# Taking the token mean off the residual input: VectorE in three operations instead of GpSimd in seven

## The chip, the cores and the metric

The kernel runs on one core of one Trainium2 chip. What counts is the device time of one execution in microseconds (us), taken as the median of several runs. The core's engines each work through their own queue in order: TensorE (PE in the profile) multiplies matrices into PSUM, VectorE (DVE) and ScalarE (ACT) do element-wise work and reductions, GpSimd (POOL) does element-wise work too, and SyncE (SP) issues most of the DMA transfers. They wait for each other through semaphores.

## The reference, cut to what matters

Two decoder layers run over 256 tokens of 1024 features. Each has three sub-layers: a feed-forward block, a mixer, and a second feed-forward block. The mixer of the first layer ("even") runs a recurrent block and gated linear attention side by side; that of the second ("odd") is latent attention. After every sub-layer the input, scaled by ALPHA, is added to the gated output, and the sum is normalised over the features of each token.

```python
def layer_norm(x, g, b):
    mu = jnp.mean(xf, -1, keepdims=True)
    var = jnp.mean(jnp.square(xf - mu), -1, keepdims=True)
    return ((xf - mu) * lax.rsqrt(var + LN_EPS) * g + b).astype(x.dtype)

def deepnorm_residual(x, f, gate, g, b, weight=1.0):
    return layer_norm(DN_ALPHA * x + weight * (1 + gate[:, None, :]) * f, g, b)
...
for l in range(DEPTH):
    mod = c_act @ mod_w[l] + mod_b[l]
    sh1, sc1, g1, sh2, sc2, g2, sh3, sc3, g3 = jnp.split(mod, N_MOD, axis=-1)
    f = swiglu(modulate(x, sh1, sc1), ffn_in[l, 0], ffn_out[l, 0])
    x = deepnorm_residual(x, f, g1, ln_g[l, 0], ln_b[l, 0], 0.5)
    u = modulate(x, sh2, sc2)
    m = even_mixer(u, ...) if l % 2 == 0 else odd_mixer(u, positions, ...)
    x = deepnorm_residual(x, m, g2, ln_g[l, 1], ln_b[l, 1])
    f = swiglu(modulate(x, sh3, sc3), ffn_in[l, 1], ffn_out[l, 1])
    x = deepnorm_residual(x, f, g3, ln_g[l, 2], ln_b[l, 2], 0.5)
```

A layer norm gives the same result when any one number per token is first taken off all of that token's features. The kernel uses this: the number is the mean over the first 128 features, so that the squares it sums later are of small numbers.

## The kernel before, in words

**Layout.** Features lie on the 128 partitions and tokens along the free axis, so that the 1024 features are eight feature tiles of 128 x 256. `ax` holds the eight tiles of the scaled input, `yy` the eight tiles of the sum.

**Weights and products.** All weights come as one stream of 1 MB slabs (`wraw`), loaded by SP in the order in which TensorE uses them. Half a slab, 128x1024, is split for precision into a high part `whi` on ScalarE (L348) and a low part `wlo` on VectorE (L349), some four half slabs ahead of use. A product of one 128x128 weight block is three matmuls of 256 columns: high with high (L420), low activation with high weight (L421), high activation with low weight (L422). Half a slab thus feeds 24 matmuls. Between the splits VectorE also reduces slabs of the conditioning weights, half a slab each (`junk`, L398); they come in through the same buffers (`modw`).

**The end of a sub-layer** is the class `Boundary`, six times in the program. `f` counts the output tiles 0 to 7.

- L610 in `tile_out` reads a finished tile from PSUM, multiplies it by the gate and adds `ax` of that tile (VectorE). This frees the PSUM bank. L614 squares the result on ScalarE, L617 and L618 add tile and square to running sums on VectorE, and L584 (ScalarE) and L585 (VectorE) make a scaled high and low copy, `flat`, which the first matmuls of the next sub-layer ("early" ones) take before the statistics are known.
- `shift_out` is called halfway through the products of tile 1, when tile 0 has been added up. L593 rounds tile 0, an all-ones matmul (L595) gives each token its mean over tile 0, L598 copies that to `shift`, and from then on it must come off everything: off `yy` tile 0 by VectorE (L601) and off `ax` tiles 1 to 7 by GpSimd (L600), so that the sums of tiles 1 to 7 lack it as they are formed. L610 of tile f therefore waits for the subtraction of tile f.
- `stats` closes the boundary: two all-ones matmuls over the running sums (L626, L627) and two over tile 7 and its square (L628, L629).

**Three kinds of boundary.** A feed-forward output tile takes 22 products, 66 matmuls, so its tiles come slowly (four boundaries). In the odd mixer a tile takes 8 products, 24 matmuls. In the even mixer the eight tiles were half summed up earlier and lie two to a PSUM bank (`acc[f]`), and 8 products finish each.

**What sets the order.** A tile scheduler places the instructions on each engine from the data they need and from priorities; everything in the boundary quoted below stands under `tc.high_priority()`. Each engine then takes its own list in order, whatever is ready further back.

```python
yr = T(wk, [P, SEQ], F32R, tag="shift", bufs=1)        # L591
act.activation(yr, y, AF.Copy)                          # L593
pe.matmul(sp[:, :SEQ], ones_r, yr, start=True, stop=True)   # L595
act.activation(shift, sp[:, :SEQ], AF.Copy)             # L598
```

Of the kernel before, what the change touches and what calls it, by code (L numbers as in the profile page):

```python
# [16 lines left out]
AF = mybir.ActivationFunctionType  # L17
DVE, ACT, PE = mybir.EngineType.DVE, mybir.EngineType.Activation, mybir.EngineType.PE
ALU = mybir.AluOpType
MULT, ADD, SUB, MAX, MIN = ALU.mult, ALU.add, ALU.subtract, ALU.max, ALU.min  # L20

P = 128
DM = 1024
KD = DM // P
SEQ = 256
# [209 lines left out]
def trunk_kernel(ctx: ExitStack, tc: tile.TileContext, xT, cvec, pos, wst, modw, colsd,  # L235
                 rgw, wa2, outT):
    nc = tc.nc
    sync, act, vec, pool, pe = nc.sync, nc.scalar, nc.vector, nc.gpsimd, nc.tensor
# [10 lines left out]
    wk = ctx.enter_context(tc.tile_pool(name="wk", bufs=2))  # L249
# [6 lines left out]
    def nm(s):  # L256
        uid[0] += 1
        return f"{s}_{uid[0]}"

    def T(pl, shape, dt=F32, tag=None, **kw):  # L260
        return pl.tile(shape, dt, tag=tag, name=nm(tag), **kw)
# [12 lines left out]
    def axps():  # L274
        return T(ps_ax, [P, 512], tag="ax")
# [192 lines left out]
    ax = T(main, [P, KD, SEQ], tag="ax")  # L468
# [73 lines left out]
    class Boundary:  # L542
# [44 lines left out]
        def shift_out(self):  # L587


            y = self.y[:, 0, :]  # L590
            yr = T(wk, [P, SEQ], F32R, tag="shift", bufs=1)  # L591
            with tc.high_priority():
                act.activation(yr, y, AF.Copy)  # L593
            sp = axps()
            pe.matmul(sp[:, :SEQ], ones_r, yr, start=True, stop=True)  # L595
            shift = T(wk, [P, SEQ], tag="shift", bufs=1)
            with tc.high_priority():
                act.activation(shift, sp[:, :SEQ], AF.Copy)  # L598
                for j in range(1, KD):
                    pool.tensor_tensor(ax[:, j, :], ax[:, j, :], shift, SUB)  # L600
                vec.tensor_tensor(y, y, shift, SUB)  # L601
                ysq = T(wk, [P, SEQ], tag="ysq")
                act.activation(ysq, y, AF.Square)
                self.scaled(0)
            self.p0 = (y, ysq)

# [745 lines left out]
```

## Time and profile before

| | us |
|---|---|
| median of three runs | 1032.38 (1031.18, 1032.38, 1034.73) |
| the profiled execution | 1033.28 |
| its span, first to last instruction | 1031.5 |
| TensorE busy | 1001.4 |
| VectorE busy | 887.0 |
| ScalarE busy | 606.2 |
| GpSimd busy | 54.7 |

The mean granted TensorE clock over the span was 0.992.

How to read the lines that follow. In the list of groups a line gives the line of the program, the engine, the operation, the output and the inputs with their shapes, and behind the bar the busy time, the mean duration of one in ns, and the idle time of the engine ahead of them. In a timeline a line starts with start and duration in us; `x2` says that two neighbours are drawn as one, and a bracket gives the idle time ahead and what ended it. A line of a table by stretches (it starts with from:to) gives the length of the stretch and then the busy time of PE, PEld (loading of weights into TensorE), DVE, ACT, POOL and SP with their counts, the granted clock, the share of time in which the DMA engines were busy, and their GB/s. In these lines the buffers' numbers are left out, so that `mm`, a PSUM bank, does not say which tile.

### The profile page before, as it was taken

The numbers are of one execution on the slowest core, as the hardware profiler recorded it, in microseconds if no ns is written. First come the engines' busy times: TensorE is split into PE (matmuls) and PEld (weight loads), VectorE is DVE, ScalarE is ACT, GpSimd is POOL, SyncE is SP. The second block draws the span as 40 slices with busy tenths as digits, with TensorE's granted clock in tenths as the row PEclk, the third lists the DMA queues.
The fourth block names the chain that finished last, engine by engine and source line by source line (L and its number), as shares of the span: only waits on it lengthen the run. The fifth ranks groups of instructions, "written<-read, shape, count | busy, mean of one in ns | idle before, by whom it ended". The sixth has DMA issues, their size and how long they took to land.

```text
span 1031.5 us, 20651 instructions
## 1 busy us (share of the span) xinstructions
PE 1001.4 (97%) x8346; PEld 978.3 (95%) x8346; DVE 887.0 (86%) x1498; ACT 606.2 (59%) x1014; POOL 54.7 (5%) x70
## 2 busy tenths in 40 slices
PE   8999999999999989999999999999999999999995
PEld 6999999998989979999999999999999889999995
DVE  5889999798999789999897899999888799666664
ACT  3646664678886656645545674454568666545442
POOL 0000011000000020000030000003000200000200
PEclk9999999999999999999999999999999999999998
DMA  9998798655566924799976479987743236666411
GB/s 345 415 349 323 272 347 313 232 203 193 196 247 258 346 98 170 261 377 377 363 290 251 165 261 371 344 330 324 286 164 123 83 127 255 237 240 244 166 41 41
DMA packets 38578, 258.57 MB, mean 251 GB/s; under 512 B 4289, under 2 KB 6849, under 8 KB 7762
## 3 DMA queue, kind: packets, MB, share of 16 engines
q1 hardware_dynamic: 37330, 256.20, 66.3%
q8 instruction: 65, 1.06, 0.4%
q10 hardware_dynamic: 1152, 1.05, 0.3%
q14 instruction: 31, 0.25, 0.1%
HBM read 256.18 MB, written 1.05 MB: 249 GB/s over the span
## 4 chain that ended last, share of the span: by engine, by line
PE 82%; DVE 11%; ACT 3%; issue 2%; DMA 2%; POOL 0%; SPq 0%; ACTq 0%; DVEq 0%
PE mm L420 25%; PE mm L422 25%; PE mm L421 25%; DVE wlo L349 3%; DVE junk L398 2%; DMA rgt<-rgw 1%; DMA wraw<-modw 1%; PE mm L1022 1%; PE mm L1021 1%; PE mm L1023 1%; ACT whi L348 1%; PE ax L422 1%; PE ax L421 1%; PE ax L420 1%; DVE acc L618 0%
## 5 line engine op out<-in xcount | busy, mean ns | idle before, releaser
L349 DVE TENSOR_TENSOR wlo<-wraw,whi 128x1024 fp32r<-128x1024 f32 x338 | 412.1, 1228 | 76.4 <-ACT whi L348 75.5
L420 PE MATMUL mm<-uhi,whi 128*128 128x256 f32 x1660 | 458.3, 278 | 7.9 <-ACT whi L348 3.6
L421 PE MATMUL mm<-ulo,whi 128*128 128x256 f32 x1660 | 458.7, 277 | 0.5 <-DVE ulo L463 0.5
L422 PE MATMUL mm<-uhi,wlo 128*128 128x256 f32 x1660 | 456.4, 277 | 0.5 <-DVE wlo L349 0.5
L348 ACT ACTIVATE whi<-wraw 128x1024 fp32r<-128x1024 f32 x338 | 353.6, 1056 | 171.9 <-PE mm L421 139.0
L420 PEld LDWEIGHTS mm<-uhi,whi 128*128 128x128 f32 x1660 | 311.3, 188 | 9.9 <-ACT whi L348 4.4
L421 PEld LDWEIGHTS mm<-ulo,whi 128*128 128x128 f32 x1660 | 312.3, 188 | 1.0 <-DVE ulo L463 0.7
L422 PEld LDWEIGHTS mm<-uhi,wlo 128*128 128x128 f32 x1660 | 311.5, 188 | 0.8 <-DVE wlo L349 0.7
L422 PE MATMUL mm<-hhi,wlo 128*128 128x256 f32 x704 | 194.5, 276 | 0.8 <-DVE wlo L349 0.8
L421 PE MATMUL mm<-hlo,whi 128*128 128x256 f32 x704 | 194.3, 276 | 0.0
L420 PE MATMUL mm<-hhi,whi 128*128 128x256 f32 x704 | 194.3, 276 | 0.0
L398 DVE CUSTOM_DVE_ANT_0 junk<-wraw,cact,cols 128x1024 bf16<-128x1024 f32 x144 | 186.4, 1294 | 7.3 <-DMA wraw<-modw 6.7
L422 PEld LDWEIGHTS mm<-hhi,wlo 128*128 128x128 f32 x704 | 132.2, 188 | 1.0 <-DVE wlo L349 1.0
L420 PEld LDWEIGHTS mm<-hhi,whi 128*128 128x128 f32 x704 | 132.2, 188 | 0.0
L421 PEld LDWEIGHTS mm<-hlo,whi 128*128 128x128 f32 x704 | 132.2, 188 | 0.0
L600 POOL TENSOR_TENSOR ax<-ax,shift 128x256 f32<-128x256 f32 x42 | 47.9, 1173 | 840.8 <-ACT shift L598 667.2
L462 ACT ACTIVATE hhi<-h 128x256 fp32r<-128x256 f32 x88 | 35.7, 413 | 61.2 <-DVE h L731 60.9
L614 ACT ACTIVATE ysq<-yy 128x256 f32<-128x256 f32 x42 | 17.4, 414 | 60.8 <-DVE yy L610 58.8
L610 DVE SCALAR_TENSOR_TENSOR yy<-mm,gate,ax 128x256 f32<-128x256 f32 x48 | 22.9, 478 | 17.7 <-PE mm L422 16.5
L731 DVE SCALAR_TENSOR_TENSOR h<-mm,sg 128x256 f32<-128x256 f32 x75 | 30.8, 416 | 8.1 <-PE mm L422 8.1
L463 DVE TENSOR_TENSOR hlo<-h,hhi 128x256 fp32r<-128x256 f32 x88 | 35.8, 415 | 0.0
L442 ACT ACTIVATE sg<-mm 128x256 f32<-128x256 f32 x75 | 27.5, 367 | 4.2 <-PE mm L422 3.0
(296 smaller groups left out, 1103.4 us busy)
## 6 DMA issues: line engine op xcount, KB each, us to landing
wraw<-wst SPq DMA_DIRECT2D x169, 1024.0 KB, 5.2
wraw<-modw SPq DMA_DIRECT2D x71, 1024.0 KB, 7.1
wraw<-modw SPq DMA_DIRECT2D x2, 512.0 KB, 5.3
rgt<-rgw ACTq DMA_DIRECT2D x8, 128.0 KB, 4.6
yy<-xT SPq DMA_DIRECT2D x8, 128.0 KB, 9.2
wraw<-wst SPq DMA_DIRECT2D x2, 512.0 KB, 6.4
outT<-yy SPq DMA_DIRECT2D x3, 256.0 KB, 2.7
outT<-yy SPq DMA_DIRECT2D x2, 128.0 KB, 2.7
```

The lines of the kernel that those rows point to most:

```text
L348: act.activation(hi, raw, AF.Copy)
L349: i = vec.tensor_tensor(lo, raw, hi.bitcast(F32), SUB)
L398: i = vec.tensor_tensor_reduce(junk, t, cact, 1.0, col("mod_b", (l * NMOD + v) * KD + j), MULT, ADD, self.modcols[(l, v)][:, j:j + 1])
L420: pe.matmul(ps, hi, mh, start=start, stop=False, skip_group_check=shared)
L421: pe.matmul(ps, hi, ml, start=False, stop=False, skip_group_check=shared)
L422: pe.matmul(ps, lo, mh, start=False, stop=stop, skip_group_check=shared)
L442: i = act.activation(out, in_, func, **kw)
L462: act.activation(hi, src, AF.Copy)
L463: return vec.tensor_tensor(lo, src, hi.bitcast(F32), SUB)
L600: pool.tensor_tensor(ax[:, j, :], ax[:, j, :], shift, SUB)
L610: vec.scalar_tensor_tensor(y, ps, self.gate[:, f:f + 1], ax[:, f, :], MULT, ADD)
L731: vec.scalar_tensor_tensor(h, pu, bu, sg, ADD, MULT)
```

## The change

In `shift_out` the seven GpSimd operations on `ax` tiles 1 to 7 become three on VectorE: one on tile 1, one on tiles 2 to 4, one on tiles 5 to 7. For several tiles at once `shift` is read again for each tile, by a broadcast view. The subtraction on `yy` tile 0 and its square now stand behind the first of the three. Nothing else in the text differs; the six boundaries all change alike. GpSimd loses 42 instructions and VectorE gains 18.

```diff
@@ -596,11 +596,13 @@
             shift = T(wk, [P, SEQ], tag="shift", bufs=1)
             with tc.high_priority():
                 act.activation(shift, sp[:, :SEQ], AF.Copy)
-                for j in range(1, KD):
-                    pool.tensor_tensor(ax[:, j, :], ax[:, j, :], shift, SUB)
-                vec.tensor_tensor(y, y, shift, SUB)
-                ysq = T(wk, [P, SEQ], tag="ysq")
-                act.activation(ysq, y, AF.Square)
+                for a, b in ((1, 2), (2, 5), (5, KD)):
+                    vec.tensor_tensor(ax[:, a:b, :], ax[:, a:b, :],
+                                      shift.rearrange("p (o s) -> p o s", o=1).broadcast_to([P, b - a, SEQ]), SUB)
+                    if a == 1:
+                        vec.tensor_tensor(y, y, shift, SUB)
+                        ysq = T(wk, [P, SEQ], tag="ysq")
+                        act.activation(ysq, y, AF.Square)
                 self.scaled(0)
             self.p0 = (y, ysq)
```

Two lines more stand ahead of all that follows, so that in the changed kernel L601 is L603, L610 is L612, L614 is L616, L617 and L618 are L619 and L620, and L626 to L629 are L628 to L631. The scheduler orders the engines anew. Three places on VectorE:

The end of the first feed-forward block, VectorE before. `rg_sp` are tiny operations of the next mixer's preparation, `junk` the reductions, and the split `wlo_1960` is the one that TensorE waits for in this stretch.

```order
L398 ISA junk_1813,mod_4_302_1804<-wraw_1800,cact_96,cols_97 128x1024
L398 ISA mod_4_302_1804 128x1
L601 TENSOR_TENSOR yy_1798<-yy_1798,shift_1973 128x256
L815 TENSOR_TENSOR rg_sp_294_1762<-rg_sp_294_1762,rg_z_1764 128x8
L398 ISA junk_1815,mod_4_302_1804<-wraw_1800,cact_96,cols_97 128x1024
L816 TENSOR_SCALAR rg_sp_294_1762<-rg_sp_294_1762 128x8
L349 TENSOR_TENSOR wlo_1960<-wraw_1698,whi_1959 128x1024
L610 SCALAR_TENSOR_TENSOR yy_1798<-mm_1922,gate_1796,ax_138 128x256
```

The same place of the change:

```order
L600 TENSOR_TENSOR ax_138<-ax_138,shift_1973 128x256
L603 TENSOR_TENSOR yy_1798<-yy_1798,shift_1973 128x256
L600 TENSOR_TENSOR ax_138<-ax_138,shift_1973 128x768 x2
L612 SCALAR_TENSOR_TENSOR yy_1798<-mm_1922,gate_1796,ax_138 128x256
L817 TENSOR_TENSOR rg_sp_294_1762<-rg_sp_294_1762,rg_z_1764 128x8
L398 ISA junk_1815,mod_4_302_1804<-wraw_1800,cact_96,cols_97 128x1024
L398 ISA mod_4_302_1804 128x1
L619 TENSOR_TENSOR acc_1799<-yy_1798 128x256
L620 TENSOR_TENSOR acc_1799<-ysq_1977,ysq_2018 128x256
```

The split `wlo_1960` is the fifth row behind these; the third reduction stands between. So the three subtractions, L610 of tile 1 with its two sums (L612, L619, L620 now) and a third reduction come ahead of that split, where before only L601, two reductions and small operations did.

The end of the even mixer, VectorE before. `mm_4260` holds tiles 0 and 1, `mm_4261` tiles 2 and 3, `mm_4262` tiles 4 and 5, `mm_4263` tiles 6 and 7; in the changed kernel they are `mm_4256` to `mm_4259`. `wlo_4653` is a split for tile 6, `wlo_4690` the next.

```order
L349 TENSOR_TENSOR wlo_4653<-wraw_4350,whi_4652 128x1024
L601 TENSOR_TENSOR yy_4229<-yy_4229,shift_4622 128x256
L610 SCALAR_TENSOR_TENSOR yy_4229<-mm_4261,gate_4227,ax_138 128x256
L610 SCALAR_TENSOR_TENSOR yy_4229<-mm_4260,gate_4227,ax_138 128x256
L349 TENSOR_TENSOR wlo_4690<-wraw_4408,whi_4689 128x1024
L617 TENSOR_TENSOR acc_4230<-yy_4229 128x256
L618 TENSOR_TENSOR acc_4230<-ysq_4632,ysq_4646 128x256
L617 TENSOR_TENSOR acc_4230<-acc_4230,yy_4229 128x256
L585 SCALAR_TENSOR_TENSOR flat_699_4255<-yy_4229,A_4243,flat_698_4254 128x256
L618 TENSOR_TENSOR acc_4230<-acc_4230,ysq_4681 128x256
L610 SCALAR_TENSOR_TENSOR yy_4229<-mm_4261,gate_4227,ax_138 128x256
```

The same place of the change:

```order
L349 TENSOR_TENSOR wlo_4645<-wraw_4346,whi_4644 128x1024
L600 TENSOR_TENSOR ax_138<-ax_138,shift_4618 128x256
L603 TENSOR_TENSOR yy_4225<-yy_4225,shift_4618 128x256
L612 SCALAR_TENSOR_TENSOR yy_4225<-mm_4256,gate_4223,ax_138 128x256
L600 TENSOR_TENSOR ax_138<-ax_138,shift_4618 128x768
L619 TENSOR_TENSOR acc_4226<-yy_4225 128x256
L612 SCALAR_TENSOR_TENSOR yy_4225<-mm_4257,gate_4223,ax_138 128x256
L620 TENSOR_TENSOR acc_4226<-ysq_4622,ysq_4638 128x256
L612 SCALAR_TENSOR_TENSOR yy_4225<-mm_4258,gate_4223,ax_138 128x256
L619 TENSOR_TENSOR acc_4226<-acc_4226,yy_4225 128x256
L600 TENSOR_TENSOR ax_138<-ax_138,shift_4618 128x768
L620 TENSOR_TENSOR acc_4226<-acc_4226,ysq_4673 128x256
```

Tile 1 now comes ahead of tile 2, and tile 4 (`mm_4258`) is evicted ahead of tile 3. The split that was fifth in the first list, now called `wlo_4682`, comes only behind L612 of tile 5, ten rows after the last one shown, and `wlo_4717` four rows after that. TensorE's list changes with it: before, it goes from 6 matmuls of tile 4 to tile 3; now it does 21 of tile 4 and one of tile 6 first, then the 24 of tile 3, then tile 5, then tiles 6 and 7.

The end of the odd mixer, VectorE before. Each tile has a bank of its own: `mm_10432` tile 0, `mm_10462` tile 1, `mm_10518` tile 2.

```order
L610 SCALAR_TENSOR_TENSOR yy_10413<-mm_10432,gate_10411,ax_138 128x256
L349 TENSOR_TENSOR wlo_10466<-wraw_9965,whi_10465 128x1024
L601 TENSOR_TENSOR yy_10413<-yy_10413,shift_10488 128x256
L610 SCALAR_TENSOR_TENSOR yy_10413<-mm_10462,gate_10411,ax_138 128x256
L585 SCALAR_TENSOR_TENSOR flat_1680_10427<-yy_10413,A_10415,flat_1679_10426 128x256
L617 TENSOR_TENSOR acc_10414<-yy_10413 128x256
L349 TENSOR_TENSOR wlo_10520<-wraw_9965,whi_10519 128x1024
L618 TENSOR_TENSOR acc_10414<-ysq_10498,ysq_10512 128x256
L610 SCALAR_TENSOR_TENSOR yy_10413<-mm_10518,gate_10411,ax_138 128x256
```

The same place of the change:

```order
L612 SCALAR_TENSOR_TENSOR yy_10397<-mm_10416,gate_10395,ax_138 128x256
L349 TENSOR_TENSOR wlo_10450<-wraw_9949,whi_10449 128x1024
L600 TENSOR_TENSOR ax_138<-ax_138,shift_10472 128x256
L603 TENSOR_TENSOR yy_10397<-yy_10397,shift_10472 128x256
L600 TENSOR_TENSOR ax_138<-ax_138,shift_10472 128x768
L612 SCALAR_TENSOR_TENSOR yy_10397<-mm_10446,gate_10395,ax_138 128x256
L600 TENSOR_TENSOR ax_138<-ax_138,shift_10472 128x768
L619 TENSOR_TENSOR acc_10398<-yy_10397 128x256
L620 TENSOR_TENSOR acc_10398<-ysq_10476,ysq_10492 128x256
L585 SCALAR_TENSOR_TENSOR flat_1680_10411<-yy_10397,A_10399,flat_1679_10410 128x256
L612 SCALAR_TENSOR_TENSOR yy_10397<-mm_10498,gate_10395,ax_138 128x256
```

The split `wlo_10520`, now `wlo_10500`, has gone from ahead of tile 2's eviction to the fifth row behind the last one shown. On SP, the load of the token positions (L483), which writes into the buffer of `shift` and has to wait for its last reader, stands five weight loads earlier in the queue than before.

## The prediction

> **What bounds the kernel now.** I read the page first, then the granted clock stretch by stretch, then TensorE's waits and the chain of waits around the six places where the token mean is taken off.
>
> ```profile
> PE 1001.4 (97%) x8346; PEld 978.3 (95%) x8346; DVE 887.0 (86%) x1498; ACT 606.2 (59%) x1014; POOL 54.7 (5%) x70
> L600 POOL TENSOR_TENSOR ax<-ax,shift 128x256 f32<-128x256 f32 x42 | 47.9, 1173 | 840.8 <-ACT shift L598 667.2
> L349 DVE TENSOR_TENSOR wlo<-wraw,whi 128x1024 fp32r<-128x1024 f32 x338 | 412.1, 1228 | 76.4 <-ACT whi L348 75.5
> ```
>
> TensorE (PE) is busy 1001.4 of 1031.5 us, so all that any edit can win is in its 30 us of idle time and in time at a low clock. The 42 GpSimd (POOL) subtractions that the change takes out are a twentieth of a span, and by themselves nobody's bound. What they do to VectorE (DVE) is the point:
>
> ```profile
> 149.67 0.15 DVE L815 TENSOR_TENSOR rg_sp<-rg_sp,rg_z 128x8 f32<-128x8 f32 x1
> 150.88 0.70 DVE L816 TENSOR_SCALAR rg_sp<-rg_sp 128x8 f32<-128x8 f32 x1
> 154.76 1.84 DVE L398 CUSTOM_DVE_ANT_0 junk<-wraw,cact,cols 128x1024 bf16<-128x1024 f32 x1
> 158.90 1.27 DVE L398 CUSTOM_DVE_ANT_0 junk<-wraw,cact,cols 128x1024 bf16<-128x1024 f32 x1
> ...
> 526.65 0.42 DVE L601 TENSOR_TENSOR yy<-yy,shift 128x256 f32<-128x256 f32 x1 [0.22 <-ACT shift L598]
> ...
> 373.30 0.97 DVE L601 TENSOR_TENSOR yy<-yy,shift 128x256 f32<-128x256 f32 x1
> ...
> L618 DVE TENSOR_TENSOR acc<-acc,ysq 128x256 f32<-128x256 f32 x30 | 12.6, 419 | 0.8
> L618 DVE TENSOR_TENSOR acc<-ysq,ysq 128x256 f32<-128x256 f32 x6 | 4.6, 762 | 0.0
> ```
>
> Before GpSimd's first subtraction a tiny 128x8 operation takes 0.15 us, during the subtractions 0.70; the reduction takes 1.84 instead of 1.27; L601 0.97 instead of 0.42; the first squared sum (x6, near the subtractions) has a mean of 762 ns where the later ones (x30) have 419. So while GpSimd subtracts, most VectorE instructions are held about 0.55 us each, whatever their size. That is the price of seven cheap subtractions.
>
> Where does it reach TensorE? At the end of the even mixer first:
>
> ```profile
> 373.02 1.84 POOL ax L600 x2
> ...
> 374.88 0.87 DVE L610 SCALAR_TENSOR_TENSOR yy<-mm,gate,ax 128x256 f32<-128x256 f32 x2 [0.62 <-POOL ax L600]
> ...
> 375.42 0.39 PE L420 MATMUL mm<-uhi,whi 128*128 128x256 f32 x1 [1.19 <-DVE yy L610]
> ...
> 380.68 0.28 PE L420 MATMUL mm<-uhi,whi 128*128 128x256 f32 x1
> 380.79 0.28 PE L421 MATMUL mm<-ulo,whi 128*128 128x256 f32 x1
> 383.00 0.38 PE L420 MATMUL mm<-uhi,whi 128*128 128x256 f32 x1 [1.93 <-DVE yy L610]
> ...
> 381.00:384.50 3.50, 1.57 (x13) 1.51 (x13) 3.50 (x11) 2.58 (x5) 0.00 (x0) 1.00 0.00 0
> 384.50:387.90 3.40, 3.40 (x18) 3.40 (x17) 2.65 (x3) 0.82 (x1) 0.00 (x0) 0.50 0.31 75
> ```
>
> Two feature tiles share a PSUM bank there, so TensorE may not start the second half of a bank before VectorE has read the first (L610). L610 waits 0.62 us for GpSimd's second tile, TensorE 1.19 us for L610; then VectorE, slowed, is late again and TensorE waits 1.93 us. Right after that the granted clock (the number ahead of the DMA share in the last two rows) is 0.50 for 3.4 us: another 3.40/2 = 1.7 us. This place loses 1.19 + 1.93 + 1.7 = 4.8 us.
>
> Then the end of the odd mixer:
>
> ```profile
> 815.61 0.42 DVE L601 TENSOR_TENSOR yy<-yy,shift 128x256 f32<-128x256 f32 x1
> 816.67 0.48 DVE L610 SCALAR_TENSOR_TENSOR yy<-mm,gate,ax 128x256 f32<-128x256 f32 x1 [0.64 <-POOL ax L600]
> ...
> 818.43 1.76 DVE L349 TENSOR_TENSOR wlo<-wraw,whi 128x1024 fp32r<-128x1024 f32 x1
> ...
> 824.62 0.47 DVE L610 SCALAR_TENSOR_TENSOR yy<-mm,gate,ax 128x256 f32<-128x256 f32 x1
> ...
> 835.10 0.48 DVE L585 SCALAR_TENSOR_TENSOR flat<-yy,A,flat 128x256 fp32r<-128x256 f32 x1
> 835.50 0.48 DVE L610 SCALAR_TENSOR_TENSOR yy<-mm,gate,ax 128x256 f32<-128x256 f32 x1
> ...
> 833.85 0.67 PE L626 MATMUL ax<-acc,ones_dm 128*128 128x256 f32 x2 [1.34 <-DVE acc L617]
> 835.23 1.22 PE L627 MATMUL ax<-acc,ones_dm 128*128 128x256 f32 x2 [0.71 <-DVE acc L618]
> ...
> 837.32 1.06 PE L629 MATMUL ax<-ysq,ones_dm 128*128 128x256 f32 x2
> ...
> 838.39 0.34 PE L422 MATMUL mm<-flat,wlo 128*128 128x258 f32 x1
> ...
> 835.00:838.40 3.40, 3.17 (x9) 2.51 (x10) 1.46 (x4) 1.58 (x5) 0.00 (x0) 0.51 0.36 152
> ```
>
> TensorE has its eight tiles done at 833.85 - 1.34 = 832.5, but VectorE evicts the last one only at 835.50; it fell behind under the subtractions (a split, L349, took 1.76 us) and, with one split and five small operations per tile, never caught up. The clock halves here too. Third, in the first feed-forward block:
>
> ```profile
> 162.13 1.21 DVE L349 TENSOR_TENSOR wlo<-wraw,whi 128x1024 fp32r<-128x1024 f32 x1
> ...
> 163.40 0.38 PE L422 MATMUL mm<-hhi,wlo 128*128 128x256 f32 x1 [0.85 <-DVE wlo L349]
> ```
>
> The other three feed-forward boundaries have no TensorE wait to win: the first of them shows 50.00 busy in 50.00 us.
>
> ```profile
> 525.00:575.00 50.00, 50.00 (x440) 49.81 (x438) 40.28 (x54) 25.16 (x34) 8.68 (x7) 1.00 0.67 250
> 400.00:525.00 125.00, 125.00 (x1103) 124.95 (x1103) 120.36 (x194) 70.07 (x110) 0.00 (x0) 1.00 0.88 330
> ```
>
> **The change part by part.** Removed: six times seven GpSimd operations, with the holds. Added to VectorE: six times one operation of 256 and two of 768 elements, the operand `shift` repeated over the tiles. No trace row has that shape; the nearest:
>
> ```profile
> L463 DVE TENSOR_TENSOR hlo<-h,hhi 128x256 fp32r<-128x256 f32 x88 | 35.8, 415 | 0.0
> L936 DVE TENSOR_TENSOR lb<-last,bc 128x512 f32<-128x512 f32 x1 | 0.7, 684 | 0.0
> ...
> 160.10 0.41 DVE L617 TENSOR_TENSOR acc<-yy 128x256 f32<-128x256 f32 x1
> 160.44 0.41 DVE L618 TENSOR_TENSOR acc<-ysq,ysq 128x256 f32<-128x256 f32 x1
> ```
>
> From 415 ns at 256 and 1228 at 1024 (L349), 768 elements come to 415 + 512 x 1.06 = 957 ns; L936, which has a repeated operand, costs 684 at 512, so repeating is free. Neighbours overlap by 0.07 us (160.10 to 160.44 for 0.41), so in the queue I count 0.34 for a small tensor operation, 0.40 for L610 and L585 (835.10 to 835.50), 1.15 for L349 and 0.88 for the new 768. Bounds for the last: 0.62 (the 512 row less the overlap) and 1.02 (three small ones). Per boundary 0.34 + 2 x 0.88 = 2.1 us are added; five to seven holds of 0.55, 2.7 to 3.9 us, go, L601's among them.
>
> *First block.* From 150.88 to the split at 162.13 VectorE took 11.25 us. Six holds of 0.55 and a smaller one (0.15) fall out, 3.4 us, and 2.1 come in: the split starts at 160.8, 1.3 earlier, more than the 0.85 that TensorE waited. But its predecessor now stands behind the three new operations, L612 and a second reduction: 150.88 plus 3 x 1.20 (reductions, 158.90 to 160.10), 2 x 0.34 + 2 x 0.88 for the subtractions, 0.40, 2 x 0.34 and some 0.5 of tiny ones is 158.5, done at 159.7, and TensorE wants it one half slab (24 matmuls of 0.114, 2.7 us) before 162.5, at 159.8. That is met with nothing to spare; I allow 0.1 lost. Gain 0.8 us (bounds 0 to 1.0).
>
> *Even mixer.* VectorE starts the new block at 373.30, when L601 starts now; the mean is there. By the new order: 0.34, 0.34, L612 for tile 1 0.40, 0.88, 0.34, then L612 for tile 2 from 375.6 to 376.1. TensorE, which in the new order first does 15 more matmuls of tile 4 and one of tile 6 past its old stopping point (375.42 - 1.19 = 374.2, less the pipeline's 0.2), comes there at 375.9: wait 0.2 instead of 1.19. Tile 4's L612 follows at 376.3, long before TensorE needs its bank (24 matmuls later, 378.9): the 1.93 goes. But ahead of the second next split in the queue now stand all operations of tiles 2 to 5: from 376.73, 0.34 + 0.88 + 0.34 + 3 x 0.40, 0.80, four sums 1.36, 0.80, the next split 1.15, 0.68, 0.40, and the split itself end at 385.9. TensorE (71 matmuls from 376.1, then four that need no low half) is there at 384.7: a new wait of 1.2 us. That leaves 4.8 - 0.2 - 1.2 = 3.4 us. Bounds: 4.8, and 1.7 if the new wait brings the low clock. Going on to tile 7 the same way gives 389.1 where the statistics (L626) now start at
>
> ```profile
> 393.05 0.59 PE L626 MATMUL ax<-acc,ones_dm 128*128 128x256 f32 x2
> ```
>
> which is 3.9, less two early matmuls not yet done, 3.7. I take 3.6.
>
> *Odd mixer.* From 815.61: 0.34, 0.34, 0.88, 0.40, 0.88, two sums 0.68, 0.40, L612 for tile 2 0.40, 0.40, 0.68, 0.40, one split 1.15: L612 for tile 3 starts at 822.6, against 824.62, but one split fewer is done by then. From there to tile 7: four L612 and four L585 at 0.40, five splits 5.75, eight sums 2.72, 11.7 us: 834.2 to 834.3, against 835.50. The sums of tile 6 are now ready when TensorE ends at 832.5, so L626 and L627 (0.43 each) and four early matmuls follow at once; it waits under 1 us for tile 7 and its square (0.42 on ScalarE), and resumes at 835.5 instead of 838.39 with two more early matmuls done: 3.1 us, of which 1.4 is the low clock. I take 3.0 (bounds 1.3 and 4.0).
>
> The low clock is weighed as the rows have it: 1.93 idle in 3.5 us, and 1.34 + 0.71, are followed by 0.50; 1.19 alone was not. [...] Without the two clock terms the sum would be 4.3 us.
>
> Moved too: the position load on SP's queue, now ahead of five weight loads and behind the third boundary's subtractions; the load after it needs a buffer that a later split frees, so nothing is added.
>
> **Sum.** 0.8 + 3.6 + 3.0 = 7.4 us off the profiled 1033.28 (span 1031.5 and 1.8 around it) is 1025.9; that execution lies 0.9 over the median, so against 1032.38 I predict 1025.0.
>
> **Rivals.** (1) *The low clock stays* in both places: 7.4 - 1.7 - 1.4 = 4.3, 1028.1. For it: short waits remain at both, 1.2 and 1 us; against: 1.19 did not drop it. (2) *The gain is given back* in the block after the even mixer, where VectorE is busy 120.36 of 125 us: if it doesn't start earlier there, up to 2.5 of 3.6 us return as split waits: 1027.5. Against: its first work there follows the statistics and moves with them. (3) *Same*: the holds were slack, and the reordered queue makes waits as long as those it removes; for it, the 1.2 us that I found myself; 1031.5. (4) *Slower*: in the even mixer VectorE's queue is in order, and the third squared sum waits for ScalarE, which may stand behind a weight conversion whose buffer TensorE frees only after tile 3 (378.9). Then VectorE idles 2.4 us, the split ends at 388.3 and TensorE waits 3.6 us and gets the low clock, 1.7: 5.5 with the 0.2, against 4.8 now. With the tight split of the first block lost as well (1 us more than hoped, nothing won) and the odd drop left with its lag (0): 1033.1. It decides from a split 1.8 us later than I count. Against: in the new order tile 4's weights are freed first, at 375.9.
>
> **How the numbers follow.** Forecast 0.56, rival 1 0.13, rival 2 0.10, rival 3 0.14, rival 4 0.07. What this kernel's measurement can tell from no change is about 0.3%, 3.1 us. The first three cases are faster by more: 0.79, and with the margins 0.79 stands; same 0.15 (rival 3 and a part of 4), slower 0.06. The range reaches down to 1022.3 (no new wait in either mixer: 1.4 + 1.0 and rounding) and up to 1030.2 (rivals 1 and 2 together).
>
> **What would show it.** Right: no 0.70 us tiny operations left; L600 on VectorE about 0.41 and 0.95 us; both 0.50 stretches gone; TensorE's largest wait in the even mixer near 1 us, on a split, not on L612; the odd mixer's L612 for tile 7 about 1.3 us sooner against L595. Wrong: a 768 operation near 1.5 us; a 0.50 stretch still there; waits of two microseconds on a split in the first or the even block.

## The result, and the profile after

The changed kernel takes 1025.3 us in the median of six runs (1024.32 to 1025.80), against 1032.59 for the kernel before in six runs (1030.89 to 1036.07): a ratio of 0.9927, 95% interval 0.9912 to 0.9942, so 6.0 to 9.1 us faster. On another occasion the same two kernels took 1026.13 and 1031.22 us (ratio 0.9946, 0.9933 to 0.9960), 5.1 us apart; the section on the low clock says why the gain differs. The profiled execution took 1024.92 us with a span of 1023.2, against 1033.28 and 1031.5 before.

The page of the changed kernel, engines and the costliest VectorE group, then the list of groups by form at the new lines:

```profile
PE 997.8 (98%) x8346; PEld 975.8 (95%) x8346; DVE 881.6 (86%) x1516; ACT 607.4 (59%) x1014; POOL 6.8 (1%) x28
L349 DVE TENSOR_TENSOR wlo<-wraw,whi 128x1024 fp32r<-128x1024 f32 x338 | 409.6, 1221 | 75.3 <-ACT whi L348 74.7
...
L600 DVE TENSOR_TENSOR ax<-ax,shift 128x768 f32<-128x768 f32 x12 | 11.1, 952 | 0.0
L600 DVE TENSOR_TENSOR ax<-ax,shift 128x256 f32<-128x256 f32 x6 | 2.5, 421 | 0.2 <-ACT shift L598 0.2
L603 DVE TENSOR_TENSOR yy<-yy,shift 128x256 f32<-128x256 f32 x6 | 2.5, 419 | 0.0
```

VectorE has 18 instructions more, 13.6 us of work more (11.1 + 2.5), and is yet busy for 5.4 us less (887.0 to 881.6): so some 19 us of what counted as its work before was waiting inside its instructions. TensorE's idle time fell by 4.7 us, from 30.1 to 25.4; the other 3.6 us of the 8.3 us of span are close to the 3.4 us that, by estimate, two stretches of 3.4 us at a clock of 0.50 cost, which are gone.

Where the time came from is read by following one matmul through both timelines. TensorE, before and then after; the rows of the two lists are the same instructions, and the third of the second list stands against L626 at 393.05 us, which the prediction shows:

```profile
19.41 0.38 PE L420 MATMUL mm<-uhi,whi 128*128 128x256 f32 x1 [1.60 <-ACT whi L348]
361.67 0.30 PE L1081 MATMUL ax<-ident,on 128*128 128x128 f32 x1 [0.45 <-DVE ut L1083]
788.33 0.30 PE L1203 MATMUL mm<-ident,e 128*128 128x128 f32 x1 [0.57 <-DVE e L1195]
```

```profile
19.19 0.39 PE L420 MATMUL mm<-uhi,whi 128*128 128x256 f32 x1 [1.43 <-ACT whi L348]
360.44 0.30 PE L1083 MATMUL ax<-ident,on 128*128 128x128 f32 x1 [0.45 <-DVE ut L1085]
387.91 0.59 PE L628 MATMUL ax<-acc,ones_dm 128*128 128x256 f32 x2
783.18 0.30 PE L1205 MATMUL mm<-ident,e 128*128 128x128 f32 x1 [0.53 <-DVE e L1197]
```

The lead is 0.22 us at the start of the weight stream (nothing of the change has run by then), 1.23 before the end of the even mixer, 5.14 at that mixer's statistics, 5.15 ahead of the odd mixer's end, and 8.3 at the last instruction. So the first block gave 1.0, the end of the even mixer 3.9, the two feed-forward boundaries behind it nothing, the odd mixer and what follows 3.15.

VectorE and TensorE at the end of the even mixer, after:

```profile
372.08 0.42 DVE L600 TENSOR_TENSOR ax<-ax,shift 128x256 f32<-128x256 f32 x1
372.42 0.42 DVE L603 TENSOR_TENSOR yy<-yy,shift 128x256 f32<-128x256 f32 x1
372.75 0.48 DVE L612 SCALAR_TENSOR_TENSOR yy<-mm,gate,ax 128x256 f32<-128x256 f32 x1
373.15 0.95 DVE L600 TENSOR_TENSOR ax<-ax,shift 128x768 f32<-128x768 f32 x1
...
383.31 1.22 DVE L349 TENSOR_TENSOR wlo<-wraw,whi 128x1024 fp32r<-128x1024 f32 x1
...
384.59 0.39 PE L422 MATMUL mm<-flat,wlo 128*128 128x258 f32 x1 [0.90 <-DVE wlo L349]
```

No operation in these rows is held any longer, and TensorE's waits of 1.19 and 1.93 us on L610 are gone. In their place stands one of 0.90 us on a split. The odd mixer's end, after, TensorE and VectorE, and a stretch of both mixers with the granted clock:

```profile
828.88 0.47 DVE L612 SCALAR_TENSOR_TENSOR yy<-mm,gate,ax 128x256 f32<-128x256 f32 x1
...
829.41 0.70 PE L630 MATMUL ax<-yy,ones_dm 128*128 128x256 f32 x2 [0.67 <-DVE yy L612]
...
385.00:388.40 3.40, 3.40 (x30) 3.35 (x30) 3.40 (x6) 1.23 (x3) 0.00 (x0) 1.00 0.77 275
831.00:834.40 3.40, 3.40 (x30) 3.40 (x30) 3.21 (x10) 3.16 (x5) 0.00 (x0) 1.00 0.00 0
```

Waits of 1.34 and 0.71 us have become one of 0.67, and the clock behind both places is full.

### The profile page after: what moved, and what is told of

Same layout as the page of the kernel before. It is cut to its first block, busy times and chain, and to the rows that moved or that the text cites. A ratio compares the mean times of both kernels' runs of the same rounds, so it can differ in the third digit from the quotient of the medians.

```text
span 1023.2 us, 20564 instructions
## 1 busy us (share of the span) xinstructions
PE 997.8 (98%) x8346; PEld 975.8 (95%) x8346; DVE 881.6 (86%) x1516; ACT 607.4 (59%) x1014; POOL 6.8 (1%) x28
## 4 chain that ended last, share of the span: by engine, by line
PE 85%; DVE 9%; DMA 2%; ACT 2%; issue 1%; ACTq 0%; DVEq 0%
PE mm L421 26%; PE mm L420 25%; PE mm L422 25%; DVE wlo L349 2%; DMA rgt<-rgw 1%; DVE junk L398 1%; DMA wraw<-wst 1%; ACT whi L348 1%; PE mm L1023 1%; PE mm L1024 1%; PE mm L1025 1%; PE ax L421 1%; PE ax L420 1%; PE ax L422 1%; DVE flat L585 1%
## 5 line engine op out<-in xcount | busy, mean ns | idle before, releaser
L398 DVE CUSTOM_DVE_ANT_0 junk<-wraw,cact,cols 128x1024 bf16<-128x1024 f32 x144 | 184.3, 1280 | 10.4 <-DMA wraw<-modw 9.8
L616 ACT ACTIVATE ysq<-yy 128x256 f32<-128x256 f32 x42 | 17.3, 414 | 42.0 <-DVE yy L612 41.8
L612 DVE SCALAR_TENSOR_TENSOR yy<-mm,gate,ax 128x256 f32<-128x256 f32 x48 | 23.0, 480 | 15.6 <-PE mm L422 15.6
L420 PE MATMUL mm<-flat,whi 128*128 128x258 f32 x96 | 28.4, 296 | 0.0
```

Source lines behind the costliest of these rows:

```text
L398: i = vec.tensor_tensor_reduce(junk, t, cact, 1.0, col("mod_b", (l * NMOD + v) * KD + j), MULT, ADD, self.modcols[(l, v)][:, j:j + 1])
L420: pe.matmul(ps, hi, mh, start=start, stop=False, skip_group_check=shared)
L612: vec.scalar_tensor_tensor(y, ps, self.gate[:, f:f + 1], ax[:, f, :], MULT, ADD)
```

## The experiments

The theory was that GpSimd's subtractions hold VectorE's instructions, and that TensorE waits for VectorE at three places out of six. Rival A put the gain down to the new order of VectorE's queue, or to a subtraction that is ready sooner than GpSimd made it.

### GpSimd busy beside the changed kernel

```diff
+    spare = T(main, [P, SEQ], BF16, tag="spare")
...
                 act.activation(shift, sp[:, :SEQ], AF.Copy)
+                for j in range(1, KD):
+                    pool.tensor_tensor(spare, shift, shift, SUB)
                 for a, b in ((1, 2), (2, 5), (5, KD)):
```

> The changed kernel, with seven GpSimd subtractions of shift from shift into a spare tile beside it at every boundary, which nobody reads. Theory (VectorE is held while GpSimd runs): VectorE's order is that of the change, but small operations take 0.70 us again and splits 1.76 us beside the seven; five to seven holds of 0.55 us, about 3 us, per boundary; TensorE's wait on a split in the even mixer grows from 1.07 us to 3 or more with the low clock (1.7 us) behind it, some 3 us come back in the odd mixer and about 1 in the first block: 1032 us (1029 to 1036). Rival A (the gain is the new order, or that a subtraction is ready sooner than GpSimd made it): 1025.3 us, within 1.

Measured: 1033.78 us, ratio to before 1.000 (0.9978 to 1.0022). VectorE's order is that of the change but for one scaled copy and one subtraction that changed places in the even mixer. VectorE and TensorE in the first block:

```profile
151.03 0.58 DVE L822 TENSOR_SCALAR rg_sp<-rg_sp 128x8 f32<-128x8 f32 x1
...
153.47 0.83 DVE L607 TENSOR_TENSOR yy<-yy,shift 128x256 f32<-128x256 f32 x1
154.22 2.65 DVE L604 TENSOR_TENSOR ax<-ax,shift 128x768 f32<-128x768 f32 x2
...
162.20 0.39 PE L422 MATMUL mm<-hhi,wlo 128*128 128x256 f32 x1 [2.21 <-DVE wlo L349]
...
379.02 0.38 PE L420 MATMUL mm<-uhi,whi 128*128 128x256 f32 x1 [1.34 <-DVE yy L616]
389.14 0.39 PE L422 MATMUL mm<-flat,wlo 128*128 128x258 f32 x1 [1.32 <-DVE wlo L349]
```

The 8-element operation takes 0.58 us, the subtraction from tile 0 takes 0.83 instead of 0.42, the pair of 768 takes 2.65 where the changed kernel's takes 1.82. TensorE waits in the first block and twice in the even mixer, and in the odd one for 1.50 and 0.98 us. Work that nobody reads takes the whole gain away, so rival A falls as the whole cause: the gain needed GpSimd to be still. Time and sign came out as the theory had them, the places only in part: the wait on a split in the even mixer grew to 1.32 us and not to 3, with another of 1.34 on an eviction, the wait in the first block is 2.21 us where about 1 was expected, and the profiled execution, the fastest of the twelve at 1031.53 us, has no low clock at all. How much a late subtraction adds of itself stays open: before the change L610 waited 0.62 us for GpSimd's second tile, and here VectorE's own subtractions are held and so late too. A hold is 0.41 us here and not 0.55, with a GpSimd operation that reads one tile twice and writes bf16.

### The mixers alone, and the feed-forward blocks alone

```diff
+                if self.s == 1:
                     for a, b in ((1, 2), (2, 5), (5, KD)):
                         vec.tensor_tensor(ax[:, a:b, :], ...
+                else:
+                    for j in range(1, KD):
+                        pool.tensor_tensor(ax[:, j, :], ax[:, j, :], shift, SUB)
```

(and with `self.s != 1` for the other kernel).

> The change at the two mixers alone, the four feed-forward boundaries as before. Theory: the first block's 1.1 us comes back, nothing else: 1026.4 us (1025.8 to 1027.2). Rival B (all six boundaries contribute, VectorE being busy everywhere): two thirds of the gain go, 1030 us.

> The change at the four feed-forward boundaries alone, the two mixers as before. Theory: only the first block's wait goes, 1.1 us: 1031.5 us (1030.5 to 1032.2). Rival B: 1028 us.

Measured: the mixers alone 1027.16 us, ratio 0.9950 (0.9927 to 0.9973); the feed-forward blocks alone 1031.06, ratio 0.9990 (0.9964 to 1.0015). Most of the gain comes from two of the six boundaries, as the theory had it, and rival B falls; the traces of before and after put it at 7.0 of 8.1 us. The gain of the feed-forward blocks is too small for these times to show, since their interval contains 1, but with the mixers alone the old wait of the first block is there again:

```profile
163.27 0.39 PE L422 MATMUL mm<-hhi,wlo 128*128 128x256 f32 x1 [0.83 <-DVE wlo L349]
```

### How a hold depends on the cut of GpSimd's work

The kernel before, with GpSimd's work in three operations, and in fourteen:

```diff
-                for j in range(1, KD):
-                    pool.tensor_tensor(ax[:, j, :], ax[:, j, :], shift, SUB)
+                for a, b in ((1, 2), (2, 5), (5, KD)):
+                    pool.tensor_tensor(ax[:, a:b, :], ax[:, a:b, :],
+                                      shift.rearrange(...).broadcast_to([P, b - a, SEQ]), SUB)
```

```diff
                 for j in range(1, KD):
-                    pool.tensor_tensor(ax[:, j, :], ax[:, j, :], shift, SUB)
+                    for h in (slice(0, SEQ // 2), slice(SEQ // 2, SEQ)):
+                        pool.tensor_tensor(ax[:, j, h], ax[:, j, h], shift[:, h], SUB)
```

> The kernel before, with GpSimd's seven subtractions put into three, over 1, 3 and 3 tiles, still on GpSimd. Theory (a hold meets every VectorE instruction that falls into GpSimd's busy time, however that is cut up): holds as before, and the eviction of tile 2 waits until all of tiles 2 to 4 are done, some 2 us later in the even mixer: 1034 us (1032 to 1037). Rival C (one hold for each GpSimd instruction): three holds instead of seven, about half of the gain, 1029 us.

> The kernel before, with each of GpSimd's subtractions cut into two of 128 elements; VectorE's and TensorE's orders are those of before. Theory G (GpSimd and VectorE take turns, and VectorE waits out the GpSimd operation that runs: 0.55 us at 256 elements, 1.65 at 768): holds of about 0.28 us, twice as many, 3.9 us in sum or less: 1032 us (1029.5 to 1034.5). Rival H (a fixed price of 0.55 us for each turn): holds stay 0.55 us and are twice as many, 7.7 us per boundary, 1036 us or more.

Measured: 1033.53 us, ratio 1.0010 (0.9987 to 1.0032), with three; 1032.90, ratio 1.0006 (0.9986 to 1.0026), with fourteen. With three, TensorE's first wait in the even mixer is 1.83 us instead of 1.19, since tile 2's subtraction ends later, and the second, of 1.93, is gone. VectorE in the first block, with three:

```profile
151.69 0.70 DVE L817 TENSOR_SCALAR rg_sp<-rg_sp 128x8 f32<-128x8 f32 x1
152.30 2.94 DVE L398 CUSTOM_DVE_ANT_0 junk<-wraw,cact,cols 128x1024 bf16<-128x1024 f32 x1
...
155.17 2.05 DVE L602 TENSOR_TENSOR yy<-yy,shift 128x256 f32<-128x256 f32 x1
```

and with fourteen:

```profile
151.93 0.44 DVE L817 TENSOR_SCALAR rg_sp<-rg_sp 128x8 f32<-128x8 f32 x1
152.28 1.56 DVE L398 CUSTOM_DVE_ANT_0 junk<-wraw,cact,cols 128x1024 bf16<-128x1024 f32 x1
...
153.77 0.67 DVE L602 TENSOR_TENSOR yy<-yy,shift 128x256 f32<-128x256 f32 x1
```

Undisturbed, the reduction takes 1.27, L601 (here L602) 0.42 and the tiny one about 0.15. So an operation is held 0.55 us beside a GpSimd operation of 256 elements, 1.67 and 1.63 beside one of 768, and 0.28, 0.29 and 0.25 beside one of 128. Rival C was right that there are about as many holds as GpSimd operations, but each lasts the longer the wider the operation is. In the first block's rows the three holds add up to 0.55 + 1.67 + 1.63 = 3.85 us; the kernel before, with seven operations, has six holds of 0.55 and one of 0.15, some 3.5 us, and the one with fourteen has thirteen of about 0.27, also some 3.5. So the theory written for three operations, that the cut makes no difference to a hold, was wrong though its time came out. Rival H (a fixed price for each turn) falls, and theory G stands as to the lengths: the holds grow with the GpSimd operation, 0.25 to 0.29, 0.55 and 1.63 to 1.67 us for 128, 256 and 768 elements. That VectorE waits out the whole operation was the author's reading and is not shown: 0.55 us is less than the 0.72 us that the shortest GpSimd subtraction of 256 took before the change. Nor does a run show what the two engines wait for in each other. Cutting GpSimd's work differently bought nothing here, by the ratios of 1.0010 and 1.0006.

### What the three operations themselves cost

```diff
-                for a, b in ((1, 2), (2, 5), (5, KD)):
-                    vec.tensor_tensor(ax[:, a:b, :], ax[:, a:b, :], ...
```

> The changed kernel without the subtractions from ax: the token mean comes off tile 0 alone, so tiles 1 to 7 of every sum keep it, and the output is not the reference's. It frees 2.1 us of VectorE at each boundary and tells what the three operations themselves cost. Theory (VectorE's time counts only where TensorE waits for it): the waits of 0.2 and 1.07 us in the even mixer and most of 0.85 us in the odd go, the rest is hidden: 1023.6 us (1022.6 to 1024.8). Rival D (VectorE, at 86%, sets the end at every boundary): six times 2.1 us, 1013 us.

Measured: 1024.68 us (fastest 1023.75), ratio to before 0.9906 (0.9879 to 0.9933). Six times 2.1 us of VectorE taken away win little. Against the changed kernel's 1025.3, measured on another occasion, it is 0.6 us; by the two ratios, 0.9906 and 0.9927, it would be 2.2, since the kernel before took 1034.07 us on this occasion. So 1.7, which was expected, is neither confirmed nor refuted, and the time lies in the range given. Rival D falls: VectorE at 86% doesn't set the end. In the even mixer one wait is left, on an eviction:

```profile
382.30 0.39 PE L420 MATMUL mm<-uhi,whi 128*128 128x256 f32 x1 [0.23 <-DVE yy L608]
```

> The change with seven VectorE operations of 256 instead of three. Theory: 7 x 0.34 = 2.4 us against 2.1, so 0.3 us more at each boundary and that seen only in the mixers, with the order about the same: 1025.8 us (1025 to 1027). Rival E (what counts is that the subtractions are few): 1028 us or more.

```diff
-                for a, b in ((1, 2), (2, 5), (5, KD)):
+                for a, b in [(j, j + 1) for j in range(1, KD)]:
```

Measured: 1026.74 us, ratio 0.9931 (0.9904 to 0.9957); within the range expected, and the grouping matters little. The other order of the queue shows at the start of the next sub-layer, with a wait that the changed kernel doesn't have:

```profile
398.49 0.74 PE L420 MATMUL mm<-uhi,whi 128*128 128x256 f32 x4 [1.43 <-ACT uhi L689]
```

### Can the new wait on the split be removed too?

Three kernels put the scaled copies later, so that the split comes sooner. The edit moves both halves of a copy, L584 on ScalarE as well as L585 on VectorE. The three are: all of tiles 1 to 7; the same with subtractions of 1, 1 and 5 tiles; and tiles 1 to 4 alone.

```diff
                     vec.tensor_tensor(self.acc[:, 1, :], p[1], ysq, ADD)
-                self.scaled(f)
+            self.scaled(f)
```

```diff
-                for a, b in ((1, 2), (2, 5), (5, KD)):
+                for a, b in ((1, 2), (2, 3), (3, KD)):
```

```diff
                     vec.tensor_tensor(self.acc[:, 1, :], p[1], ysq, ADD)
-                self.scaled(f)
+                if f > 4:
+                    self.scaled(f)
+            if f <= 4:
+                self.scaled(f)
```

> The change, with the scaled copies of tiles 1 to 7 (L585) taken out of the high priority. In the even mixer the split that TensorE waits for stands right behind the eviction of tile 3, some 2 us sooner. Theory (the new wait is one of order alone): the 1.07 us go, 1024.3 us (1023.7 to 1025.2). Rival F (VectorE is full from 370 to 390 us, and what is put off comes due at the statistics): 1025.3 us, within 0.4.

> The kernel of the scaled copies put later, with the subtractions grouped 1, 1 and 5 tiles instead of 1, 3 and 3, so that the eviction of tile 2 in the even mixer waits for 0.5 us less. Theory: the 0.2 us wait there goes too, 1024.1 us (1023.5 to 1025). Rival F: 1025.3 us, within 0.4.

> The change, with the scaled copies of tiles 1 to 4 alone taken out of the high priority (those of tiles 5 to 7 stay in it). In the even mixer the split that TensorE waits for stands right behind the eviction of tile 3, and behind the statistics the order is that of the change. Theory (both waits, 1.07 us on the split and 1.8 us at the next sub-layer's start, are order): neither is there, 1.0 us under the changed kernel run beside it. Rival F (what is put off comes due at the statistics): within 0.4 us of it or slower.

> The changed kernel once more, to stand beside the kernel with the scaled copies of tiles 1 to 4 put later: 1025.3 us (1024.5 to 1026.5), with a wait of 1.07 us on the split.

Measured: 1026.37 us for the first and 1025.98 for the second (ratios to before 0.9924, 0.9900 to 0.9949, and 0.9924, 0.9899 to 0.9949), and, beside one another, 1026.48 for the third and 1026.13 for the changed kernel (0.9965, 0.9948 to 0.9981, and 0.9946, 0.9933 to 0.9960). None is clearly faster than the change, and the first two lie above the ranges of theory and rival alike. In them the wait on the split is gone, as the theory had it, but TensorE waits 1.65 us at the start of the next sub-layer. TensorE in the third:

```profile
384.75 0.39 PE L422 MATMUL mm<-flat,wlo 128*128 128x258 f32 x1 [0.48 <-DVE wlo L349]
396.24 0.74 PE L420 MATMUL mm<-uhi,whi 128*128 128x256 f32 x4 [1.43 <-ACT uhi L692]
```

Here the wait on the split is halved, and 1.43 us of waiting appear at the first input of the next sub-layer. ScalarE there, in the third kernel and then in the changed one:

```profile
393.45 1.05 ACT L348 ACTIVATE whi<-wraw 128x1024 fp32r<-128x1024 f32 x1
394.74 1.06 ACT L348 ACTIVATE whi<-wraw 128x1024 fp32r<-128x1024 f32 x1 [0.23 <-PE mm L421]
395.70 0.49 ACT L692 ACTIVATE uhi<-ut,B 128x256 fp32r<-128x256 f32 x1
```

```profile
393.01 1.05 ACT L348 ACTIVATE whi<-wraw 128x1024 fp32r<-128x1024 f32 x1
394.06 0.51 ACT L689 ACTIVATE uhi<-ut,B 128x256 fp32r<-128x256 f32 x1
```

A second weight conversion has come ahead of `uhi`, and it waits for TensorE besides; VectorE had the input of `uhi` ready at 394.47 us, 1.2 us before ScalarE took it up. So the outcome is rival F's, but by another way than it said: not VectorE's overdue work, since from the statistics to that input its order was that of the change, but ScalarE's order. Since the edit moves L584 as well, ScalarE's queue was changed by it directly; whether moving L585 alone would leave `uhi` where it was stays untested.

### Is the low clock tied to the waits?

> The kernel before once more, for its profile. Theory (the low clock behind the two waits is not fixed to them but differs from one execution to the next): the waits of 1.2 and 1.9 us in the even mixer and 1.3 and 0.7 in the odd stand again, and the granted clock of 0.50 behind them may be missing; without it the time is near 1030.2 us. Rival (a wait of this length always brings it): 0.50 at both places again.

Measured: 1032.39 us. TensorE's waits are the same to 0.01 us in this execution of the kernel before (1.19, 1.93, 1.34, 0.71). In the clock records of each trace the switches lie on multiples of 3.41 us, on a grid that stands differently to the program in each: in the profiled execution of before they are 375.47, 3.41, 447.15, 3.41 and 184.32 us apart, 110, 1, 131, 1 and 54 times 3.413, and in that of the changed kernel 1006.93, 295 times. Stretches on that grid, the one with the waits and the one behind it; first the profile shown of before, then this one, then that of the feed-forward blocks alone, whose mixers are those of before:

```profile
381.10:384.52 3.42, 1.52 (x13) 1.53 (x14) 3.42 (x10) 2.58 (x5) 0.00 (x0) 1.00 0.00 0
384.52:387.93 3.41, 3.41 (x19) 3.41 (x18) 2.63 (x3) 0.85 (x1) 0.00 (x0) 0.50 0.32 79
831.66:835.08 3.42, 1.52 (x10) 0.95 (x8) 3.39 (x7) 2.47 (x4) 0.00 (x0) 1.00 0.51 163
835.08:838.49 3.41, 3.26 (x9) 2.60 (x10) 1.39 (x5) 1.50 (x5) 0.00 (x0) 0.50 0.34 144
```

```profile
381.00:384.41 3.41, 1.48 (x13) 1.28 (x11) 3.41 (x10) 2.58 (x5) 0.00 (x0) 1.00 0.00 0
384.41:387.82 3.41, 3.41 (x19) 3.41 (x18) 2.50 (x3) 0.20 (x1) 0.00 (x0) 0.50 0.28 46
831.56:834.97 3.41, 1.98 (x14) 1.41 (x12) 3.38 (x6) 2.46 (x5) 0.00 (x0) 1.00 0.26 91
834.97:838.39 3.42, 2.70 (x15) 2.19 (x16) 2.48 (x7) 2.04 (x6) 0.00 (x0) 1.00 0.51 216
```

```profile
378.74:382.16 3.42, 1.51 (x14) 1.32 (x12) 3.42 (x10) 2.70 (x4) 0.13 (x1) 1.00 0.00 0
382.16:385.57 3.41, 3.39 (x29) 3.39 (x30) 3.41 (x6) 1.25 (x3) 0.00 (x0) 1.00 0.00 0
829.30:832.72 3.42, 1.76 (x12) 1.19 (x10) 3.38 (x7) 2.47 (x5) 0.00 (x0) 1.00 0.41 129
832.72:836.13 3.41, 2.92 (x17) 2.42 (x18) 2.47 (x8) 2.04 (x6) 0.00 (x0) 1.00 0.42 178
```

The same waits are followed by the low clock at both places, at the first alone, and at neither. The kernel with fourteen GpSimd operations had it at the second alone, with 1.51 us of TensorE work in the stretch ahead, and the one with three at both, with 1.58 and 0.96 us. With 1.75 us or more it stayed away at these places; with 1.58 or less it came six times out of seven. By an estimate from the clock of 0.50 each time costs 3.41/2 = 1.7 us, so the kernel before loses 0 to 3.4 us to it by chance; in the first stretch of the profile shown of before the matmuls start 0.21 us apart and not 0.11.

This is also why the gain differs between occasions. Profiled executions without such a stretch have a mean granted clock of 0.996 or 0.997. The executions of the kernel before at 0.996 took 1030.7 us in the median (29 of them, on three occasions); the changed kernel at 0.996 or 0.997 took 1025.3 on the first occasion (six of six) and 1026.0 on the other (three of six). So about 5 us of the gain stand without the clock, and the rest is how often the kernel before met it.

## Why the prediction was right, by its own steps

| step | predicted | measured in the profiled pair |
|---|---|---|
| first block | 0.8 us | 1.0 |
| even mixer | 3.6 | 3.9 |
| odd mixer | 3.0 | 3.15, with what follows |
| other three boundaries | 0 | 0 for two (a lead of 5.14 us at 393 and 5.15 at 788 us of before); the last is within the odd mixer's row |
| sum off the profiled execution | 7.4 | 8.1, and 0.2 at the start |
| median | 1025.0 | 1025.3 |

**The holds.** That most VectorE instructions lose about 0.55 us while GpSimd subtracts, and that this is the price of its operations, is shown by the first experiment, and by the kernels with three and fourteen operations. "Whatever their size" is right for VectorE's operations of 8, 256 and 1024 elements (0.70 against 0.15, 0.97 against 0.42, 1.84 against 1.27); the hold goes with the size of GpSimd's operation (0.25 to 0.29, 0.55 and 1.65 us for 128, 256 and 768 elements), which seven equal operations could not show.

**The price of the new operations.** 952 ns for 768 elements, against 957 worked out from 256 and 1024 elements; so the repeated operand cost nothing here.

**First block.** The 0.1 us lost on the next split didn't come, since that split started at 158.05 where 158.5 was counted; nothing took its place.

**Even mixer.** The wait of 0.2 us on L612 shows as the second of two matmuls 0.31 us behind the first instead of 0.11. The new wait on the split was put at 1.2 us and is 0.90 idle, 1.07 by the start times. That split was counted to end at 385.9 us of the old timeline; it ends at 384.53, on a timeline that runs 1.22 ahead at L600 (372.08 against 373.30), so 385.75. The walk through an in-order queue, with 0.34, 0.40, 0.88 and 1.15 us per instruction, holds to 0.2 us over 30 instructions.

**Odd mixer.** L612 for tile 7 comes 1.5 us sooner against L595 (20.62 us behind it before, 19.12 after), 1.3 was forecast. TensorE waits 0.67 us where under 1 was said.

**Two errors that cancel, and luck in the clock.** The sum was 0.7 us short. And the last step, which took 0.9 us off 1025.9 because the profiled execution lay that far over the median, was wrong: part of that excess was the low clock at two places, which the change removes and which therefore was in the sum already. Without that step 1025.9 stands against 1025.3. The clock terms, 1.7 and 1.4 us, were right for the execution shown, but a wait of that length doesn't always bring them, as the sum took for granted. Without them the sum was 4.3 us, and about 5 were measured at the full clock; that the medians of the first occasion lie 7.3 us apart, so near to 7.4, owes something to how often the low clock came to the kernel before. The upper end of the range is a slip of the sum besides: rivals 1 and 2 together, by their own terms, come to 1030.6 us and not 1030.2.

**The rivals.** The low clock didn't stay; the gain wasn't given back behind the even mixer (5.14 us of lead at its statistics, 5.15 at 788 us); the wait of rival 4 never passed 0.90 us, since ScalarE's squares came in time. What rival 2 and 3 feared, a reordered queue that makes new waits, is real: seven operations on VectorE, and each of the three kernels with the scaled copies put later, brought 1.4 us or more at the next sub-layer's start. In the changed kernel that place happens to be free.

## What to carry to other kernels

Work that was given to GpSimd to spare VectorE was not free for VectorE here: it was charged for nearly every GpSimd operation, by an estimate some 2.1 us per 1000 elements of a partition (0.55 for 256, 1.65 for 768), on most instructions that came along, where VectorE's own operation took 0.95 us for 768. Look for tiny instructions that suddenly take several times their length (here 0.70 us and not 0.15), then ask at which places the bounding engine waits behind them: here two places out of six held 7.0 of the 8.1 us. Before a second improvement on such a place, follow the queues of all engines to the next boundary, since three reorderings here only moved the wait.

## What the runs showed of the hardware

- **VectorE beside GpSimd.** Holds of 0.25 to 0.29, 0.55 and 1.65 us beside GpSimd operations of 128, 256 and 768 elements; 0.41 us beside one of 256 that reads one tile twice and writes bf16. L610, which reads PSUM, took 0.47 to 0.48 us all 48 times in the kernel before, beside GpSimd's subtractions or not, and 0.47 us beside operations of 128.
- **The low clock by chance.** Its switches lie on a grid of 3.41 us, and the same wait of 1.93 us was followed by it in two executions of the kernel before and not in that of the feed-forward blocks alone. How much TensorE worked in the stretch of the grid ahead goes with it (1.58 us or less, six times out of seven; 1.75 or more, never at these places), but does not settle it. A place that the change doesn't touch shows the same: a wait on a DMA ahead of L873 (L871 before), 1.4 to 1.9 us long in the fourteen traces, was followed by 0.50 for 6.8 us in three of them (three operations on GpSimd, no subtraction, seven operations on VectorE). In the changed kernel and in the one with seven operations it is 1.68 us long and TensorE worked 1.73 us of the stretch in both, and the clock was full behind the first and 0.50 behind the second:

```profile
296.25:299.66 3.41, 1.73 (x13) 1.51 (x12) 3.21 (x4) 0.81 (x1) 0.00 (x0) 1.00 0.96 346
299.66:303.07 3.41, 3.41 (x31) 3.36 (x30) 1.63 (x3) 2.92 (x5) 0.00 (x0) 1.00 0.86 283
```

```profile
296.95:300.36 3.41, 1.73 (x13) 1.48 (x11) 2.32 (x4) 0.42 (x2) 0.00 (x0) 1.00 0.93 314
300.36:303.77 3.41, 3.41 (x18) 3.41 (x18) 1.48 (x3) 2.68 (x5) 0.00 (x0) 0.50 0.76 296
```

  What decides at the same share of work stays open; the grid's exact edge and the ends of matmuls, which the profile models, are not known well enough to tell.
